# Order of the first loads, attention stages and last weight units in a hybrid decoder layer

## The chip, the cores and the metric

The kernel runs on one core of a Trainium2 chip. A core has a matrix engine (TensorE, PE in the profile, with its weight loads as PEld), three engines for elementwise work (VectorE or DVE, ScalarE or ACT, GpSimd or POOL), and SyncE (SP), which here issues nearly all transfers from HBM. Each engine works through its own list of instructions in order; between engines semaphores carry the dependences. The metric is the time of the kernel on the device in microseconds, lower is better.

## The reference

One decoder layer on x of 256 positions by 2048 channels, all in float32. Cut to what matters:

```python
h = rmsnorm(x, pre_mix_g)
q_a, k_a, v_a, q_b, k_b, v_b, f_b = jnp.split(h @ w_in, cuts, axis=-1)
o_a = swa_sink_attention(q_a, k_a, v_a, sinks)       # 16 heads, 2 kv heads, window 128, ALiBi
o_b = forgetting_attention(q_b, k_b, v_b, log_sigmoid(f_b + b_forget))   # 16 heads
mix = concat([rmsnorm(o_a, grp_swa_g), rmsnorm(o_b, grp_fox_g)]) @ w_out
x = x + rmsnorm(mix, post_mix_g)
h = rmsnorm(x, pre_ffn_g)
u = causal_dwconv(h @ w_up, conv_w, conv_b)          # width 3, 11264 channels
gate, val = jnp.split(u, 2, axis=-1)
x = x + rmsnorm((gelu(gate) * val) @ w_down, post_ffn_g)
```

## The kernel before, in words

**Precision.** Every matmul is done in three passes on numbers that are split in two: a rounded high part (`whi`, written by ACT) and the remainder (`wlo`, written by DVE as raw minus high). Activations are split the same way (`hT`, `G`, `oT`: columns 0 to 255 high, 256 to 511 low). The products are high by high, high by low and low by high.

**Weights.** A weight unit is 512 KB: `w_load` (line 64) starts its transfer on SyncE into one of four `raw` buffers, `w_split` (line 83) makes `whi` and `wlo` from it, five buffers each. `w_high` (line 69) does the same with the low part put off, for the places where the order is written by hand. `proj_T` (line 170) runs a projection of 256 output columns over four units; each unit is 8 matmuls of 512 columns and 8 of 256, and calls `tick` twice. `mm3` (line 197) is the three passes of the other kind of product, for one 128-row tile `t` of the positions.

**Order.** PE's instructions run in the order in which the program issues them. The other engines are put in order by a scheduler, except where an instruction is pinned (`keep_in_program_order`) or where a stretch is set to manual for ACT, DVE and POOL (line 653 to the end of `first_gate`). `later(n, f)` puts a piece of work n ticks on; it is how attention is laid among the projections.

**Start.** SyncE loads a small gain tile, then x in four chunks of 512 channels (the first in two halves), each followed by a unit of the key/value columns of group A. `x_chunk` transposes a chunk on PE and splits it into `hT`; `proj_T` with `first` then runs the key/value projection `bkv`. The squares of x for the norm are made by ACT in between. The first query projection (`g = 0`) follows as an ordinary `proj_T`. `rows_pre` turns the norm's factors into a row, by a matmul of ones with a diagonal (`row_of`, one diagonal buffer); `kv_a` makes the keys and values; both come 4 ticks after the key/value projection.

**Attention.** `attend` (line 335) handles a pair of heads in three stages, `scores` (with the softmax on DVE and ACT), `transposes` of the softmax, with the split into `ph` and `pl`, and `pv`, the product with the values. `stages` (line 457) gives their ticks, n, n + 5 and n + 7. Eight pairs of group A come first, eight of group B later, 8 ticks apart.

**Hand-over.** The output projection's second half keeps the units of its last two column chunks (`kept[2]`, in the common weight buffers, and `kept[3]`, in four buffers of their own), so that position tile 0 can be finished (`mix_rstd`, `residual`, `turn`: transposes to `hT`) while tile 1 is still being multiplied. `out_cols` runs a kept chunk for one tile; `gate_unit` fetches the four units of the MLP's first gate projection; `first_gate` runs it, `one(t, u)` for tile t and unit u. `ffn_tables` makes the norm's row for the MLP.

**End.** The down projection runs over four column chunks of 11 units in each half. In the last chunk of the second half the last 3 units multiply tile 0 first and tile 1 after it. `down` adds to `y_sb`, sums the squares and multiplies by the gain; at the end each tile gets its factor, is added to `x_sb` and is stored, all from SyncE.

## Time and profile before

| what | us |
|---|---|
| median of 3 runs (1118.9 to 1120.0) | 1119.46 |
| the profiled execution | 1118.4 |
| its span, first to last instruction | 1116.7 |
| PE busy | 1088.4 |
| DVE busy | 750.7 |
| ACT busy | 630.6 |
| POOL busy | 189.0 |

The span is what the trace covers; the execution's own time has another 1.7 us around it. Busy time is a union over an engine's instructions; matmuls overlap their neighbours, so PE counts as busy also where a short gap stands between two starts. In rows of the timeline the columns are start, length, engine, line, operation, output <- inputs, and in brackets the idle time of the engine before it and what ended it. In the list of waits they are total, number and longest.

### The profile page before, as it was taken

What the parts mean: (1) busy time and instruction counts of PE and PEld (TensorE: products, weight loads), DVE (VectorE), ACT (ScalarE), POOL (GpSimd) and SP (SyncE); (2) the same over time, 40 slices, a digit from 0 to 9 for tenths busy, and PEclk for the clock granted to TensorE, in tenths of its full rate; (3) what the DMA queues carried; (4) which work ended last, traced back from release to release, by engine and by line L of the source; (5) the groups of instructions that cost most, each with busy time, mean ns of one, the idle gap of its engine ahead of it and who ended that gap; (6) DMA issues with size and microseconds to landing.
All of it is one profiled execution on the core that took longest, in us unless ns stands there. A gap on an engine that the chain in (4) does not pass through costs nothing.

```text
span 1116.7 us, 15954 instructions
## 1 busy us (share of the span) xinstructions
PE 1088.4 (97%) x5846; PEld 932.0 (83%) x5846; DVE 750.7 (67%) x1141; ACT 630.6 (56%) x1077; POOL 189.0 (17%) x271
## 2 busy tenths in 40 slices
PE   8999999999999999999999999999999999999995
PEld 6779988888888888888888888888888888888884
DVE  5868787888566876767676544456777677755553
ACT  6656676667555765656565444455656565644440
POOL 4333215442013111010101000001111111101111
PEclk9999999999999999999999999999999999999998
DMA  7734466554763556565656665656565655666552
GB/s 235 223 99 129 141 197 186 168 165 152 254 208 122 175 188 196 183 195 181 196 182 194 186 189 187 189 186 191 186 192 187 191 186 190 187 228 188 189 168 76
DMA packets 164842, 202.87 MB, mean 182 GB/s; under 512 B 6780, under 2 KB 130716, under 8 KB 164252
## 3 DMA queue, kind: packets, MB, share of 16 engines
q1 hardware_dynamic: 164368, 201.67, 57.5%
q8 instruction: 46, 0.75, 0.3%
q14 instruction: 32, 0.26, 0.1%
q10 hardware_dynamic: 396, 0.18, 0.1%
HBM read 199.58 MB, written 2.11 MB: 181 GB/s over the span
## 4 chain that ended last, share of the span: by engine, by line
PE 86%; DVE 5%; ACT 4%; issue 2%; POOL 1%; DMA 1%; SPq 0%; DVEq 0%; POOLq 0%; ACTq 0%
PE bank_acc L201 31%; PE bank_acc L180 21%; PE bank_att L180 13%; PE bank_acc L185 11%; PE bank_att L185 7%; DVE wlo L89 1%; ACT whi L88 1%; PE bank_att L348 1%; PE bank_att L397 1%; DVE pl L205 1%; DMA x_in<-in_x_dram 1%; PE bank_att L399 0%; ACT hT L626 0%; DVE y_sb L855 0%; PE bank_att L350 0%
## 5 line engine op out<-in xcount | busy, mean ns | idle before, releaser
L89 DVE TENSOR_TENSOR wlo<-raw,whi 128x1024 fp32r<-128x1024 f32 (+2 forms) x360 | 452.7, 1258 | 259.4 <-ACT whi L88 258.8
L88 ACT CAST whi<-raw 128x1024 fp32r<-128x1024 f32 (+2 forms) x360 | 371.0, 1032 | 272.7 <-PE bank_acc L201 141.1
L180 PE MATMUL bank_acc<-hT,whi 128*128 128x512 f32 x1152 | 295.7, 394 | 0.0
L180 PEld LDWEIGHTS bank_acc<-hT,whi 128*128 128x128 f32 x1152 | 206.1, 189 | 35.9 <-ACT whi L88 0.4
L201 PE MATMUL bank_acc<-whi,G 128*128 128x512 f32 x704 | 221.7, 395 | 0.0
L185 PEld LDWEIGHTS bank_acc<-hT,wlo 128*128 128x128 f32 x1152 | 156.9, 191 | 10.3
L185 PE MATMUL bank_acc<-hT,wlo 128*128 128x256 f32 x1152 | 161.9, 284 | 0.0
L180 PE MATMUL bank_att<-hT,whi 128*128 128x512 f32 x640 | 161.9, 392 | 0.0
L201 PEld LDWEIGHTS bank_acc<-whi,G 128*128 128x128 f32 x704 | 132.4, 188 | 31.9
L739 POOL TENSOR_TENSOR u<-u,rowf 128x256 f32<-128x256 f32 x88 | 55.4, 651 | 550.2 <-DVE u L738 545.5
L201 PE MATMUL bank_acc<-wlo,G 128*128 128x512 f32 x352 | 139.2, 396 | 0.0
L180 PEld LDWEIGHTS bank_att<-hT,whi 128*128 128x128 f32 x640 | 115.1, 189 | 20.6
L185 PEld LDWEIGHTS bank_att<-hT,wlo 128*128 128x128 f32 x640 | 87.3, 190 | 6.2
L185 PE MATMUL bank_att<-hT,wlo 128*128 128x256 f32 x640 | 89.2, 282 | 0.0
L201 PE MATMUL bank_acc<-whi,oT 128*128 128x512 f32 (+1 forms) x272 | 83.5, 384 | 0.0
L201 PEld LDWEIGHTS bank_acc<-wlo,G 128*128 128x128 f32 x352 | 66.2, 188 | 16.0
L201 PEld LDWEIGHTS bank_acc<-whi,oT 128*128 128x128 f32 x272 | 50.2, 188 | 10.6 <-ACT whi L75 0.3
L201 PE MATMUL bank_acc<-wlo,oT 128*128 128x512 f32 (+1 forms) x136 | 52.0, 382 | 1.0 <-DVE wlo L78 1.0
L201 PE MATMUL bank_acc<-whi,hT 128*128 128x384 f32 (+1 forms) x192 | 47.6, 322 | 0.0
L737 ACT COPY cs<-bank_acc 128x256 f32<-128x256 f32 x48 | 15.9, 373 | 32.7 <-PE bank_acc L180 32.7
L201 PEld LDWEIGHTS bank_acc<-whi,hT 128*128 128x128 f32 x192 | 33.7, 188 | 0.0
L201 PEld LDWEIGHTS bank_acc<-wlo,oT 128*128 128x128 f32 x136 | 25.6, 188 | 6.3 <-DVE wlo L78 1.3
(205 smaller groups left out, 992.6 us busy)
## 6 DMA issues: line engine op xcount, KB each, us to landing
raw<-in_w_up_dram SPq DMA_DIRECT2D x176, 512.0 KB, 3.5
raw<-in_w_down_dram SPq DMA_DIRECT2D x88, 512.0 KB, 4.7
raw<-in_w_in_dram SPq DMA_DIRECT2D x52, 512.0 KB, 3.7
raw<-in_w_out_dram SPq DMA_DIRECT2D x32, 512.0 KB, 4.2
raw<-in_w_in_dram SPq DMA_DIRECT2D x16, 384.0 KB, 3.2
raw<-in_w_in_dram SPq DMA_DIRECT2D x8, 272.0 KB, 2.8
cb<-c_dram SPq DMA_DIRECT2D x8, 256.0 KB, 3.6
x_sb<-in_x_dram SPq DMA_DIRECT2D x2, 1024.0 KB
```

The lines of the kernel that those rows point to most:

```text
L88: i1 = act.copy(hi[:, :n], raw[:, :n])
L89: i2 = dve.tensor_tensor(lo[:, :n], raw[:, :n], hi[:, :n].bitcast(F32), op=ALU.subtract)
L180: pe.matmul(b, hi[:, a, m * P:(m + 1) * P], hT[:, kt, :], start=(kt == 0), stop=(kt == KT - 1))
L185: pe.matmul(b[:, 256:512], lo[:, a, m * P:(m + 1) * P], hT[:, u * 4 + a, 0:256], start=False, stop=False)
L201: pe.matmul(b, a, r[:, cols], start=(first and i == 0), stop=(last and i == 2))
L205: dve.tensor_tensor(lo, src, hi.bitcast(F32), op=ALU.subtract)
L348: pe.matmul(s1, a[:, P:256], b, start=(n == 0), stop=(n == 2))
L397: pe.matmul(ov, values(hl, 0), p[:, :, 0:256], start=(n == 0), stop=False)
L737: act.copy(c, b[:, 256:512])
L739: pool.tensor_tensor(u[:, 2:258], u[:, 2:258], rowf, op=ALU.mult)
```

## The change

Four places change, beside helpers that only carry a new argument.

1. **Start.** The gain tile is loaded by ACT's queue. The first x chunk and the first key/value unit are loaded in halves that alternate; then come the first query unit and, for each further chunk, x, its key/value unit and its query unit, in pinned order. Key/value and first query projections run side by side, unit by unit: the key/value unit, then the transposes of the next x chunk, then the query unit. The key/value accumulators use banks of the attention's tag. There are two diagonal buffers, and the diagonals are made as soon as the factors are there. `warm_up(4)` becomes `warm_up(2)`.
2. **Attention.** The stages are n, n + 6 and n + 9. Group A's first scores stand 6 ticks after the queries, not 4; group A's norm comes at tick 16, not 12.
3. **Hand-over.** The own buffers hold chunk 2 and the common ones chunk 3; tile 1 is multiplied with chunk 3 first, then with chunk 2 in two halves. The low parts of the gate units and of the transposed tile are put in another order, and `one(0, 2)` stands ahead of tile 1's transposes.
4. **End.** In the last chunk six units (`HOLD`) feed tile 0 alone at first; two of them are split into buffers of their own. Tile 1's last chunk is accumulated in two halves of 256 columns in two banks, and the order from there on is written out. The sum of squares without the last part is made ahead; tile 1's stores alternate between SyncE's and ACT's queue, the last piece in 256 columns.

The core of the diff:

```diff
-        for cs in ((slice(0, 256), slice(256, 512)) if c == 0 else
-                   (slice(c * 512, (c + 1) * 512),)):
-            sp.dma_start(x_in[:, :, cs], xv[:, :, cs])
-        first.append(w_load(w_rows(w_in, c * 4, 4, 1024, 256), 4, 256))
+    for i in range(2):
+        cs = slice(i * 256, (i + 1) * 256)
+        tc.keep_in_program_order(sp.dma_start(x_in[:, :, cs], xv[:, :, cs]))
+        tc.keep_in_program_order(
+            sp.dma_start(head[:, i * 512:(i + 1) * 512].rearrange("p (a c) -> p a c", a=2),
+                         w_rows(w_in, i * 2, 2, 1024, 256)))
+    first[0].append((head, 4, 256))
+    first[1].append(w_load(w_rows(w_in, 0, 4, 0, 256), 4, 256, True))
+
+    def first_load(c):
+        cs = slice(c * 512, (c + 1) * 512)
+        tc.keep_in_program_order(sp.dma_start(x_in[:, :, cs], xv[:, :, cs]))
+        for i, c0 in enumerate((1024, 0)):
+            first[i].append(w_load(w_rows(w_in, c * 4, 4, c0, 256), 4, 256, True))
...
+        x_part(0, (0,))
+        warm_up(2)
+        bkv = [bank("att"), bank("att")]
+        bq0 = [bank(), bank()]
+        for u in range(4):
+            parts = w_split(first[0][u], True, None if u else lambda: x_part(0, (1,)))
+            if u < 2:
+                first_load(u + 2)
+            unit_T(parts, u, bkv, False, u == 0)
+            if u:
+                x_square((2, 3, 2)[u - 1])
+            parts = w_split(first[1][u], True)
+            if u == 0:
+                x_square(1)
+            if u < 3:
+                x_part(u + 1, (0, 1))
+            else:
+                for t in range(2):
...
+                    rpre.append(rstd_of(st, D, f"rpre{t}"))
+                    dpre.append(diag_of(rpre[t]))
+                later(2, rows_pre)
+            unit_T(parts, u, bq0)
...
         def stages(n):
-            return n, n + 5, n + 7
+            return n, n + 6, n + 9
...
-        later(4, kv_a)
+        kv_a()
...
-                swa_pair(2 * g + m, q_pair(b2[m]), stages(4 + 8 * (2 * g + m) - 8 * g))
+                swa_pair(2 * g + m, q_pair(b2[m]), stages(6 + 8 * (2 * g + m) - 8 * g))
...
-        later(12, lambda: group_rstd(0, rstd_a))
+        later(16, lambda: group_rstd(0, rstd_a))
...
-                (hi, lo), low = w_high(raw, hp if n == 3 else None)
+                (hi, lo), low = w_high(raw, (hp, 4) if n == 2 else None)
...
-        b12 = out_cols(2, 1, whole)
-        pairs = [turn(0, 0), turn(0, 1)]
-        for high, _ in pairs:
+        b13 = out_cols(3, 1, whole)
+        turns = [turn(0, 0), turn(0, 1)]
+        for high, _ in turns:
             high()
-        evac_b(1, 2, b12)
+        evac_b(1, 3, b13)
         lows[0]()
-        for _, low in pairs:
+        for _, low in turns:
             low()
-        evac_b(1, 3, out_cols(3, 1, slice(0, 256)), 0)
-        for high, low in (turn(0, 2), turn(0, 3)):
+        evac_b(1, 2, out_cols(2, 1, slice(0, 256)), 0)
+        lows[1]()
+        turns = [turn(0, 2), turn(0, 3)]
+        for high, _ in turns:
             high()
-            low()
-        evac_b(1, 3, out_cols(3, 1, slice(256, 512)), 1)
+        turns[0][1]()
+        evac_b(1, 2, out_cols(2, 1, slice(256, 512)), 1)
+        turns[1][1]()
         mix_rstd(1)
-        lows[1]()
         for n in range(4):
             residual(1, n)
-        lows[2]()
...
-                rffn.append(rstd_of(st2, D, f"rffn{t}"))
+                dffn.append(diag_of(rstd_of(st2, D, f"rffn{t}")))
...
+            one(0, 2)
+            for high, low in [turn(1, u) for u in range(4)]:
                 high()
                 low()
-            one(0, 2)
             one(0, 3)
+            lows[2]()
...
+        for u in range(FHALF // 2):
+            hi, lo = w_unit(w_rows(w_down, FHALF + u * 2, 2, 1536, 512), 2, 512,
+                            keep=(fp, HOLD - 4) if LAST <= u < FHALF // 2 - 4 else None)
+            for a in range(2):
+                k = u * 2 + a
+                args = (k, hi[:, a, :], lo[:, a, :])
+                held.append(args)
+                mm3(b0, G[k], 0, *args[1:], slice(0, 512), k == 0, k == FHALF - 1)
+                for h in range(2 if u < LAST else 0):
+                    mm3(b1[h][:, halves[h]], G[k], 1, *args[1:], halves[h], k == 0, False)
...
+        v = before_last(0, 3)
+        down(0, 3, b0)
+        r = rstd_y(0, 3, v)
+        for n in range(4):
+            finish(0, slice(n * 512, (n + 1) * 512), r, sp)
+        last = fp.tile([P, 256], F32, tag="last", name="last")
+        for h in range(2):
+            if h:
+                v = before_last(1, 4)
+            for k, hi, lo in held[LAST * 2:]:
+                mm3(b1[h][:, halves[h]], G[k], 1, hi, lo, halves[h], False, k == FHALF - 1)
+            down(1, 3, b1[h], h, last if h else None)
+        r = rstd_y(1, 4, v)
+        for i, n in enumerate((512, 512, 512, 256, 256)):
+            c = (0, 512, 1024, 1536, 1792)[i]
+            finish(1, slice(c, c + n), r, (sp, act)[i % 2], last if i == 4 else None)
```

Three places show what the numbers and helpers do to the engines' orders. On PE at the start of the program, of the kernel before, from the second x chunk on (`bank_acc<-hT,whi` is a high pass of the key/value projection):

```order
L225 MATMUL bank_att<-ident,x_in 128x128 x8
L180 MATMUL bank_acc<-hT,whi 128x512 x6
L185 MATMUL bank_acc<-hT,wlo 128x256 x8
L180 MATMUL bank_acc<-hT,whi 128x512 x2
```

The same engine in the changed kernel, from the second half of x chunk 0 on (`bank_att<-hT` is the key/value projection here, `bank_acc<-hT` the queries'):

```order
L260 MATMUL bank_att<-ident,x_in 128x128 x4
L203 MATMUL bank_att<-hT,whi 128x512 x4
L208 MATMUL bank_att<-hT,wlo 128x256 x4
L203 MATMUL bank_att<-hT,whi 128x512 x2
L208 MATMUL bank_att<-hT,wlo 128x256 x4
L203 MATMUL bank_att<-hT,whi 128x512 x2
L260 MATMUL bank_att<-ident,x_in 128x128 x8
L203 MATMUL bank_acc<-hT,whi 128x512 x6
L208 MATMUL bank_acc<-hT,wlo 128x256 x8
```

Before, the first unit of keys and values stood behind the transposes of chunk 1; now it stands ahead of them, in two halves, and a query unit follows them.

On DVE behind the first pair's transposes, of the kernel before (`pl` is the low part of the transposed softmax, `oT` the evacuated value product, `t1s`, `nm` the next pair's scores and row maxima):

```order
L205 TENSOR_TENSOR pl<-bank_att,ph 128x384 x2
L89 TENSOR_TENSOR wlo<-raw,whi 128x1024
L408 SCALAR_TENSOR_TENSOR oT_116<-bank_att,gcol,oT_116 64x256 x2
L353 TENSOR_TENSOR t1s<-bank_att,t1s 128x512
L354 TENSOR_TENSOR t0s<-bank_att,t0s 128x256
L357 TENSOR_REDUCE nm<-t1s 128x2
L358 TENSOR_REDUCE nm<-t0s 128x2
```

And in the changed kernel:

```order
L240 TENSOR_TENSOR pl<-bank_att,ph 128x384 x2
L399 TENSOR_TENSOR t1s<-bank_att,t1s 128x512
L400 TENSOR_TENSOR t0s<-bank_att,t0s 128x256
L403 TENSOR_REDUCE nm<-t1s 128x2
L404 TENSOR_REDUCE nm<-t0s 128x2
L100 TENSOR_TENSOR wlo<-raw,whi 128x1024
L410 TENSOR_TENSOR nm<-nm,nsnk 128x4
L411 TENSOR_TENSOR es<-nm,snk 128x4
L454 SCALAR_TENSOR_TENSOR oT_115<-bank_att,gcol,oT_115 64x256
```

The evacuation of a pair's value product has moved from ahead of the next pair's scores into that pair's softmax.

On DVE at the hand-over, of the kernel before, from the first half of tile 1's last chunk on (`hT` rows are the low parts of a transposed tile, `x_sb` the residual, the `wlo` rows the gate's low splits):

```order
L595 SCALAR_TENSOR_TENSOR mix_sb<-bank_acc,rg_3370,mix_sb 128x256
L631 SCALAR_TENSOR_TENSOR hT_3639<-bank_att,gcol,hT_3639 128x128 x8
L595 SCALAR_TENSOR_TENSOR mix_sb<-bank_acc,rg_3370,mix_sb 128x256
L609 TENSOR_REDUCE st_m<-msq_3478 128x1
L140 TENSOR_SCALAR rv<-st_m 128x1
L78 TENSOR_TENSOR wlo<-raw,whi 128x1024
L614 SCALAR_TENSOR_TENSOR x_sb<-mix_sb,rmix_3920,x_sb 128x512 x4
```

And in the changed kernel:

```order
L645 SCALAR_TENSOR_TENSOR mix_sb<-bank_acc,rg_3389,mix_sb 128x256
L87 TENSOR_TENSOR wlo<-raw,whi 128x1024
L681 SCALAR_TENSOR_TENSOR hT_3640<-bank_att,gcol,hT_3640 128x128 x4
L645 SCALAR_TENSOR_TENSOR mix_sb<-bank_acc,rg_3389,mix_sb 128x256
L681 SCALAR_TENSOR_TENSOR hT_3640<-bank_att,gcol,hT_3640 128x128 x4
L659 TENSOR_REDUCE st_m<-msq_3479 128x1
L163 TENSOR_SCALAR rv<-st_m 128x1
L664 SCALAR_TENSOR_TENSOR x_sb<-mix_sb,rmix_3922,x_sb 128x512 x4
```

The low split has moved ahead of the last quarter's evacuation, four of the eight low parts behind it, and nothing stands between the factor's sum and the residual.

More of the change, by code (lines that the diff above doesn't have):

```diff
@@ L26 @@
 FHALF = 22
+HOLD = 6
 @with_exitstack
@@ L71, in w_high @@
+    def w_high(unit, keep=None):
         raw, a, c = unit
         n = a * c
-        hi = (pool_ or wp).tile([P, UNIT], F32R, tag="whi", bufs=4 if pool_ else 5, name="whi")
-        lo = (pool_ or wp).tile([P, UNIT], F32R, tag="wlo", bufs=4 if pool_ else 5, name="wlo")
-        act.copy(hi[:, :n], raw[:, :n])
+        hi, lo = w_parts(n, keep)
+        act.copy(hi, raw[:, :n])
         def low():
-            dve.tensor_tensor(lo[:, :n], raw[:, :n], hi[:, :n].bitcast(F32), op=ALU.subtract)
-        return (hi[:, :n].rearrange("p (a c) -> p a c", a=a),
-                lo[:, :n].rearrange("p (a c) -> p a c", a=a)), low
@@ L83, in w_split @@
-    def w_split(unit, pin=False):
+            dve.tensor_tensor(lo, raw[:, :n], hi.bitcast(F32), op=ALU.subtract)
+        return [x.rearrange("p (a c) -> p a c", a=a) for x in (hi, lo)], low
+    def w_split(unit, pin=False, between=None, keep=None):
         raw, a, c = unit
         n = a * c
-        hi = wp.tile([P, UNIT], F32R, tag="whi", bufs=5, name="whi")
-        lo = wp.tile([P, UNIT], F32R, tag="wlo", bufs=5, name="wlo")
-        i1 = act.copy(hi[:, :n], raw[:, :n])
-        i2 = dve.tensor_tensor(lo[:, :n], raw[:, :n], hi[:, :n].bitcast(F32), op=ALU.subtract)
-        if pin:
-            tc.keep_in_program_order(i1)
-            tc.keep_in_program_order(i2)
-        return (hi[:, :n].rearrange("p (a c) -> p a c", a=a),
-                lo[:, :n].rearrange("p (a c) -> p a c", a=a))
@@ L166, in row_of, with unit_T, high, low @@
         return bk[:, 0:256]
-    def proj_T(w, c0, banks, loaded=None, before=None, pin=False):
+    def unit_T(parts, u, banks, ticks=True, halves=False):
+        hi, lo = parts
+        def high(a):
+            kt = u * 4 + a
+            for m, b in enumerate(banks):
+                pe.matmul(b, hi[:, a, m * P:(m + 1) * P], hT[:, kt, :], start=(kt == 0),
+                          stop=(kt == KT - 1))
+        def low(a):
+            for m, b in enumerate(banks):
+                pe.matmul(b[:, 256:512], lo[:, a, m * P:(m + 1) * P],
+                          hT[:, u * 4 + a, 0:256], start=False, stop=False)
+        high(0)
+        high(1)
+        if halves:
+            low(0)
+            low(1)
+        high(2)
+        if ticks:
+            tick()
+        for a in range(2 if halves else 0, 4):
+            low(a)
+        high(3)
+        if ticks:
+            tick()
@@ L171, in proj_T @@
+    def proj_T(w, c0, banks, before=None, pin=False):
         for u in range(4):
-            unit = loaded[u] if loaded else w_load(w_rows(w, u * 4, 4, c0, 256), 4, 256)
-            hi, lo = w_split(unit, pin and u > 0 or loaded)
+            parts = w_split(w_load(w_rows(w, u * 4, 4, c0, 256), 4, 256), pin and u > 0)
             if before:
                 before(u)
-            def high(a):
-                kt = u * 4 + a
-                for m, b in enumerate(banks):
-                    pe.matmul(b, hi[:, a, m * P:(m + 1) * P], hT[:, kt, :], start=(kt == 0),
-                              stop=(kt == KT - 1))
@@ L789, in first_gate @@
             return banks
-        ysq = [small.tile([P, 4], F32, tag=f"ysq{t}", bufs=1, name=f"ysq{t}") for t in range(2)]
+        ysq = [small.tile([P, 5], F32, tag=f"ysq{t}", bufs=1, name=f"ysq{t}") for t in range(2)]
         gbf = None
```

161 lines of the change are left out of this document (85 added, 76 removed).

## The prediction

> **What bounds the kernel now.** I read the page first, then busy time by stage, then the waits of PE, then the timeline at each place where PE stands still.
>
> ```profile
> span 1116.7 us, 15954 instructions
> PE 1088.4 (97%) x5846; PEld 932.0 (83%) x5846; DVE 750.7 (67%) x1141; ACT 630.6 (56%) x1077; POOL 189.0 (17%) x271
> ```
>
> ```profile
> 0.00:39.40 39.40, 33.77 (x180) 26.46 (x181) 24.80 (x41) 26.36 (x52) 19.09 (x40) 0.96 0.76 236
> 39.40:158.00 118.60, 112.34 (x676) 102.10 (x675) 93.27 (x196) 77.02 (x185) 33.84 (x39) 1.00 0.49 147
> 158.00:290.00 132.00, 131.48 (x730) 111.45 (x730) 106.00 (x186) 88.17 (x195) 49.61 (x74) 1.00 0.54 168
> 290.00:386.00 96.00, 92.07 (x506) 78.15 (x505) 62.69 (x101) 55.54 (x109) 19.81 (x22) 1.00 0.61 199
> 386.00:1104.80 718.80, 718.75 (x3762) 613.84 (x3760) 458.43 (x611) 382.76 (x536) 64.89 (x94) 1.00 0.59 185
> 1104.80:1116.70 11.90, 0.00 (x0) 0.00 (x0) 5.54 (x10) 0.72 (x2) 1.77 (x2) 0.59 0.49 176
> ```
>
> TensorE is busy for 97% of the span. Columns are the stretch, its length, then PE, PEld, DVE, ACT, POOL busy, clock, DMA share and GB/s. From 386 to 1104.8 us PE is busy for 718.75 of 718.80 us, and the change leaves those matmuls alone, except in the last weight column. All that can be won lies in the other five rows: the start, the two attention rows, the hand-over to the MLP, and 11.9 us after the last matmul. The waits of PE name the places (total, times, longest):
>
> ```profile
> PE bank_att L386 <- DVE t0s L376: 3.7, 3, 1.9
> PE bank_att L225 <- DMA x_in<-in_x_dram: 3.1, 1, 3.1
> PE bank_att L165 <- DVE diag L164: 2.5, 2, 1.3
> PE bank_att L397 <- DVE pl L205: 2.4, 3, 1.1
> PE bank_att L621 <- DVE x_sb L614: 1.7, 1, 1.7
> ```
>
> **The start: 5.2 us.** One weight unit of a transposed projection (8 wide and 8 narrow matmuls) takes 1.84 + 0.95 = 2.79 us:
>
> ```profile
> 161.50 1.84 PE bank_acc L180 x8
> 163.34 0.95 PE bank_acc L185 x8
> ```
>
> ```profile
> 9.96 1.09 PE L225 MATMUL bank_att<-ident,x_in 128*128 128x128 f32 x8 [3.11 <-DMA x_in<-in_x_dram]
> ...
> 38.95 2.00 PE L180 MATMUL bank_acc<-hT,whi 128*128 128x512 f32 x8
> ```
>
> ```profile
> 10.00:20.00 10.00, 10.00 (x57) 8.93 (x58) 6.38 (x11) 6.08 (x14) 4.93 (x7) 0.83 0.93 294
> GB/s 0 5 124 336 148 284 320 367 371 388 349 367 384 363 314 176 346 187 321 137 0 123 362 55 3 220 323 216 315 302 179 44 314 244 264 255 253 264 147 329
> ```
>
> Keys/values and the first queries are 8 units. Before, the second one ends with the first two matmuls of the row at 38.95, so at 39.4 us; some 1.0 us of that is small work that stays (gain rows, diagonals, value transposes): 38.4. Of the changed kernel, x and both projections are 6.3 MB. The second line gives GB/s for each us. x chunk 1 ended the first 1.57 MB of the list before and was landed by 9.96 us; now 2.1 MB end with it: 0.52 MB more at 350 to 370 GB/s is 1.4 us later, less about 0.45 us because the tiny gain load (a SyncE issue of that length) leaves the queue: 10.9 us. Unit 0 of keys/values runs before that, in two halves, on data landed by about 8 us. Behind chunk 1, PE has three transposed chunks (0.87 us each: 8 at 0.109, by the row at 9.96, whose last one runs on for 0.27) and seven units: 2.6 + 19.5 + 0.2 for joints = 22.3, done at 33.2. That is 38.4 - 33.2 = **5.2 us**. No unit waits on its own chunk: between a chunk's transposes and the unit that uses it stands the query unit of the chunk before, 2.79 us. ACT then has per chunk 1.57 (hT) + 2.1 (casts) + 0.87 a square, 5.4 to 6.3 us beside PE's 6.46; that cover is thin, and where it fails some tenths appear. SyncE gets a new wait: the load of keys/values unit 2 needs the first raw buffer, and behind it stand query unit 2, x chunk 3 and all later weights; that buffer is free near 10 us, chunk 3 then lands near 16, and PE wants it near 23. Bounds: chunk 1 landed at 9.5 (same place as before, less the gain load) gives 6.6; landed at 12.2 (0.52 MB at the row's mean of 234) gives 3.9; half clock once more costs 1.7 (below).
>
> Row 10 to 20 us has clock 0.83: after the idle 3.1 us TensorE ran half as fast for some 3.4 us, 1.7 us lost. My chain has no PE gap over 1.2 us before 11 us, so I charge none. The Trainium skill, "TensorE: Matmul & The Clock Gate", Part 1, says that the clock is halved after an idle window of about 3.4 us of a free-running counter, and its Part 4 that transposes do not count as activity in the same way. By that second rule the stretch from 4 to 8 us, which is warm-up, transposes and a small start on unit 0, could count as idle and the sum would lose 1.7 us again; before, a similar stretch kept full clock.
>
> **Attention: 7.7 us.** The sixteen pairs each put scores, transposes of the softmax and the product with the values on PE at ticks of about 1.4 us (half a unit).
>
> ```profile
> 45.00 0.40 PE L348 MATMUL bank_att<-keys,qh 128*128 128x512 f32 x1
> ...
> 53.65 0.47 DVE L376 TENSOR_SCALAR t0s<-t0s,rs 128x128 f32<-128x128 f32 x2
> ...
> 203.32 0.63 PE L397 MATMUL bank_att<-ph,vpb 128*128 128x512 f32 x2
> 204.05 0.50 PE L397 MATMUL bank_att<-pl,vpb 128*128 128x512 f32 x1
> ```
>
> Waits for the softmax (3.7) and for pl (2.4) are 6.1 us of idle PE; each of the six hides 0.16 more, as a matmul of 0.39 us is followed at a pitch of 0.23: 1.0. Five forget-gate pairs lose 204.05 - 203.32 - 0.47 = 0.26 each without showing idle: 1.3; two small ones at 85 and 100 us about 0.5. Together 8.9. The normalised softmax came 54.1 - 45.0 = 9.1 us after the scores, with 8.0 us of PE work ahead. Now 6 ticks stand there, 8.4 + 1.05 for the scores = 9.45, and from the second pair on also the previous pair's value product, 1.05: 10.5. So the softmax waits should go, even if that product's evacuation (two DVE instructions of some 0.45, four on ACT) now falls into the next softmax: 9.1 + 0.9 = 10.0. The third tick behind the transposes adds 1.4 us, and the next scores another 1.05, where the largest wait for pl was 1.1. What stays: pair 0, with no product ahead and the queries' evacuation 2 ticks behind its scores, 0.5; pair 6, whose ticks are 1.0 us, 0.3; and the first scores, which now stand 9.2 us behind the diagonals and must have keys that come by way of GpSimd, a copy through the queue and ACT, 0.4 (an estimate). 8.9 - 1.2 = **7.7**. Bounds: 8.9, and 3 if DVE, busy 93.3 of 118.6 us there, gives half of it back.
>
> **Hand-over to the MLP: 4.0 us.**
>
> ```profile
> 360.66 1.60 DVE L78 TENSOR_TENSOR wlo<-raw,whi 128x1024 fp32r<-128x1024 f32 x1
> ...
> 361.14 1.53 POOL L142 TENSOR_TENSOR rmix<-rv,mhalf 128x1 f32<-128x1 f32 x1
> ...
> 363.51 2.64 PE L621 MATMUL bank_att<-ident,x_sb 128*128 128x128 f32 x16 [1.70 <-DVE x_sb L614]
> ...
> 381.57 0.49 PE L165 MATMUL bank_att<-diag,ones 128*128 128x128 f32 x2 [1.21 <-DVE diag L164]
> ```
>
> The transposes of tile 1 wait 1.7 us for the residual and then trickle at its pace, 2.64 us for 1.74 (16 at 0.109). Ahead of that, DVE was behind with the last quarter's evacuation: eight low parts of about 0.27 us stood before it; now four do, some 1.0 us. The 1.60 us low split leaves the place between the sum and the residual, and while it ran the power on GpSimd took 1.53 us; I take back 0.9 of that (an estimate, from the 0.55 of the same line where DVE was idle). So the residual starts 1.9 us earlier, and PE has eight more matmuls, one(0,2), 0.96 us, ahead of the transposes, which then run at once: 2.5 us won. Both diagonals are now made before PE asks for them (second near 376.9, asked for near 377.5): 1.5 us. The 1.0 us wait on the kept low split at 342 us stays, as the square ahead of that cast stays. Bounds: 1.5 (one of the two) to 4.5.
>
> **The end: 3.0 us.**
>
> ```profile
> 1103.95 2.74 DVE L855 SCALAR_TENSOR_TENSOR y_sb<-y_sb,ry,x_sb 128x512 f32<-128x512 f32 x4 [1.53 <-POOL ry L142]
> ...
> 1106.61 0.68 DVE L828 TENSOR_TENSOR y_sb<-bank_acc,y_sb 128x512 f32<-128x512 f32 x1
> ...
> 1109.99 2.74 DVE L855 SCALAR_TENSOR_TENSOR y_sb<-y_sb,ry,x_sb 128x512 f32<-128x512 f32 x4 [1.50 <-POOL ry L142]
> ```
>
> ```profile
> 352.59 0.28 PE L201 MATMUL bank_acc<-wlo,oT 128*128 128x256 f32 x1
> 352.71 0.40 PE L201 MATMUL bank_acc<-whi,oT 128*128 128x256 f32 x2
> ```
>
> Tile 1's first sum is ready at 1109.99 + 0.69 = 1110.68, 5.9 us after PE, 1.8 of them because DVE still finishes tile 0 (the addition starts only at 1106.61); the output then takes 6.01 us. Now tile 0 has 72 narrow matmuls of cover, 8.6 us, for its 6.1 us chain. After the last matmul: addition of 256 columns 0.47, square and read-out 0.5, one small sum 0.16, power 0.55, first residual 0.69, hand-overs 0.2: 2.5. Since 1 MB still has to leave, I keep the 6.0: 8.5 instead of 11.9, 3.4 won. 66 wide matmuls become 132 narrow ones; a narrow one starts 0.12 us after the one before it, a wide one 0.233 (8 in 1.84 and a hand-over), so 132 x 0.12 - 66 x 0.233 = 0.4 lost. **3.0**, bounds 2 to 3.6. Weights for the six units that feed tile 0 alone (1.4 us each, 512 KB) are loaded ahead; nine units of buffers hide that, and I charge nothing (bound 1).
>
> **Sum.** 5.2 + 7.7 + 4.0 + 3.0 = 19.9. The profiled execution took 1118.4 us (span 1116.7 and 1.7 around it): 1098.5. The median of the runs shown, 1119.46, is 1.1 higher: 1099.6, say **1099.5**.
>
> **Rivals.** (1) Waits come back as DVE and ACT run nearer to full in the first 160 us: the start wins 3.5 and attention 3.5, 1105.4. For: DVE is busy 79% there; against: it idles in every stretch. (2) The clock halves again at the start, because too little of a 3.4 us stretch before 11 us is matmul: 1.7, 1101.2; the row of 10 to 20 us shows that it can, and a denser start speaks against it. (3) Slower than before: each next pair's softmax is pushed behind the previous pair's evacuation. It decides from 10.5 us between scores and softmax; at 12.2 for all sixteen, 1.7 x 16 = 27 us lost against 12.2 won elsewhere, 1134. Against: 9.1 was the most seen, forget pairs had slack. (4) Little happens, as each wait is handed on to a later one: 1118; against: 386 to 1104.8 shows PE waits for nothing there.
>
> **Chances.** Forecast 0.62 (1095.5 to 1102), clock 0.13, rival 1 0.18, no change 0.03, slower 0.04. All low bounds together would be 1112, all high ones 1096. Range 1095 to 1107, 0.85 of it. A measurement tells about 0.2% (2.2 us) from no change: faster 0.93, same 0.03, slower 0.04.
>
> **What would show it.** Right: first queries done near 33 us, clock 1.00 from 10 to 20; no PE wait for softmax or pl over 0.5 us; no wait of the transposes for x_sb or of the row for its diagonal; 8.5 us behind the last matmul. Wrong: PE waiting for casts or the chunk transposes before 33 us, or new waits of transposes near 10.5 us behind the scores.

## The result, and the profile after

| | before | after |
|---|---|---|
| median of the runs, us | 1119.61 (4 runs, 1118.9 to 1120.0) | 1103.12 (4 runs, 1100.63 to 1104.05) |
| ratio of the medians | | 0.985, 95% interval 0.9831 to 0.9869 |
| profiled execution (span), us | 1118.4 (1116.7) | 1102.26 (1100.5) |

The kernel became 1.5% faster. The forecast was 1099.5 in a range of 1095 to 1107; the measured median lies in the range, but 3.6 us above the forecast, outside the 1095.5 to 1102 that had most of the chance, and 2.3 us below the 1105.4 of rival 1. The forecast sum was 19.9 us; the spans differ by 16.2. Where the 3.7 us are missing is the question of the rest.

The head of the page of the changed kernel, then its busy time by stage; columns are the stretch, its length, PE, PEld, DVE, ACT and POOL busy, clock, DMA share and GB/s:

```profile
span 1100.5 us, 16111 instructions
PE 1083.3 (98%) x5910; PEld 935.0 (85%) x5910; DVE 751.6 (68%) x1146; ACT 630.8 (57%) x1080; POOL 196.0 (18%) x272
```

```profile
0.00:33.30 33.30, 31.69 (x172) 25.14 (x173) 19.50 (x36) 24.47 (x49) 16.64 (x38) 1.00 0.76 243
33.30:142.00 108.70, 104.87 (x640) 97.11 (x639) 91.03 (x182) 72.18 (x173) 36.78 (x40) 1.00 0.52 157
142.00:274.00 132.00, 130.32 (x738) 111.98 (x737) 109.09 (x199) 90.05 (x205) 54.71 (x74) 1.00 0.55 172
274.00:370.00 96.00, 94.97 (x523) 81.34 (x522) 62.34 (x101) 58.32 (x113) 17.29 (x21) 1.00 0.58 194
370.00:1091.20 721.20, 721.20 (x3843) 619.38 (x3843) 466.06 (x625) 385.26 (x541) 69.11 (x97) 1.00 0.58 188
1091.20:1100.50 9.30, 0.28 (x3) 0.08 (x1) 3.54 (x7) 0.51 (x2) 1.45 (x3) 0.76 0.33 114
```

The reader looks at length minus PE busy. The start now idles 1.6 us (5.6 before), the hand-over 1.0 (3.9), the middle nothing, the end 9.0 (11.9). The two attention rows still idle 3.8 and 1.7 us; before it was 6.3 and 0.5. The stretches don't hold quite the same work, so the rows only point to the place.

For equal work I use single instructions that exist in both kernels: the end of the first queries, the matmul behind the one wait that stayed (kept low split of the output projection), and the last matmul. Timeline of PE, before:

```profile
342.31 0.50 PE L201 MATMUL bank_acc<-wlo,oT 128*128 128x512 f32 x1 [1.01 <-DVE wlo L78]
...
1104.36 0.40 PE L201 MATMUL bank_acc<-whi,G 128*128 128x512 f32 x1
```

And after:

```profile
33.26 0.60 PE L191 MATMUL bank_att<-diag,ones 128*128 128x128 f32 x4
...
333.26 0.50 PE L236 MATMUL bank_acc<-wlo,oT 128*128 128x512 f32 x1 [1.03 <-DVE wlo L87]
...
1091.21 0.28 PE L236 MATMUL bank_acc<-whi,G 128*128 128x256 f32 x1
```

The kept split's wait ends 9.05 us earlier, the last matmul starts 13.15 us earlier, the span ends 16.2 us earlier. The first queries end at 33.26 (38.4 before, without the small work that stays). So:

| part | forecast, us | measured, us |
|---|---|---|
| start: 38.4 - 33.26 | 5.2 | 5.1 |
| attention: 9.05 - 5.1 | 7.7 | 3.9 |
| hand-over and narrow matmuls: 13.15 - 9.05 | 4.0 - 0.4 | 4.1 |
| end: 16.2 - 13.15 | 3.4 | 3.05 |

Three parts came as forecast and one came half. PE's waits of the changed kernel say why (total us, times, longest):

```profile
PE bank_att L432 <- DVE t0s L422: 3.8, 2, 2.4
...
PE bank_att L590 <- POOL sqs L460: 1.1, 1, 1.1
PE bank_acc L236 <- DVE wlo L87: 1.0, 1, 1.0
PE bank_att L394 <- ACT keys L239: 0.6, 1, 0.6
PE bank_att L203 <- DVE hT L178: 0.2, 1, 0.2
PE bank_att L208 <- DVE wlo L100: 0.2, 1, 0.2
```

All waits for pl are gone, and those for x_sb, the diagonals and chunk 1. But two transposes wait for their softmax, 1.4 us at pair 0 and 2.4 at pair 6, where I had left 0.5 and 0.3. Two waits are new: the group norm's matmul for the square sum on GpSimd (1.1) and the first forget-gate scores for their keys (0.6). Together that is 5.5 us.

**The 1.4 us: pair 0.** Timeline of DVE of the changed kernel; pair 0's scores run on PE from 42.69 to 43.91:

```profile
42.43 0.87 DVE L240 TENSOR_TENSOR keys<-scr,keys 64x256 fp32r<-64x256 f32 x2
...
45.21 1.22 DVE L100 TENSOR_TENSOR wlo<-raw,whi 128x1024 fp32r<-128x1024 f32 x1
46.35 0.68 DVE L399 TENSOR_TENSOR t1s<-bank_att,t1s 128x512 f32<-128x512 f32 x1
```

DVE takes the scores up 2.4 us after they are done (0.3 in the kernel before): splits of the keys and the values, a copy of gains and two low splits stand ahead of them. From the start of the scores to the end of the softmax it is 11.1 us instead of 9.1.

**The 2.4 us: pair 6.** Its scores start at 124.60; the transposes come at 135.28, 10.7 us later, while the narrow matmuls ahead of them are done at 132.9. Timeline of ACT of the changed kernel there:

```profile
123.54 0.87 ACT L239 CAST ph<-bank_att 128x384 fp32r<-128x384 f32 x2
127.81 1.05 ACT L99 CAST whi<-raw 128x1024 fp32r<-128x1024 f32 x1 [3.40 <-DMA raw<-in_w_in_dram]
130.36 1.05 ACT L99 CAST whi<-raw 128x1024 fp32r<-128x1024 f32 x1 [1.51 <-DMA raw<-in_w_in_dram]
131.32 0.46 ACT L452 ACTIVATE oT<-bank_att,gcol 64x256 fp32r<-64x256 f32 x1
131.68 0.50 ACT L415 ACTIVATE t1s<-t1s,nm 128x256 f32<-128x256 f32 x1
```

ACT stands still for 4.9 us, on two casts whose weights are still being loaded. Pair 6's exponentials (L415) are queued behind them. On DVE the last step that they need (L410, at 130.03) stands in turn behind the low split of the first of these casts.

**The 1.1 and 0.6 us: group norm and keys.** Timeline of POOL of the changed kernel:

```profile
159.66 0.48 POOL L492 TENSOR_SCALAR t1f<-cb,cq 128x256 f32<-128x256 f32 x1 [4.09 <-DMA cb<-c_dram]
...
164.48 0.73 POOL L460 TENSOR_TENSOR sqs<-sqs,sqo 128x256 f32<-128x256 f32 x1
...
167.05 2.06 POOL L165 TENSOR_TENSOR rg<-rv,mhalf 128x1 f32<-128x1 f32 x2
169.09 1.42 POOL L365 TENSOR_TENSOR scr<-scr 128x256 f32<-128x256 f32 x2
```

POOL first waits for the cumulative sums, which go through memory (cb from c_dram), makes the mask tables of the first two forget-gate pairs from 159.66 on, fits pair 7's square sum between them, then does the norm's two powers, and only then scales the keys (L365). PE waits at two points of this row.

### The profile page after: what moved, and what is told of

The parts are those of the page before. It is cut to its first block, busy times and chain, and to the rows that moved or that the text cites. A ratio compares the mean times of both kernels' runs of the same rounds, so it can differ in the third digit from the quotient of the medians.

```text
span 1100.5 us, 16111 instructions
## 1 busy us (share of the span) xinstructions
PE 1083.3 (98%) x5910; PEld 935.0 (85%) x5910; DVE 751.6 (68%) x1146; ACT 630.8 (57%) x1080; POOL 196.0 (18%) x272
## 4 chain that ended last, share of the span: by engine, by line
PE 92%; DVE 2%; ACT 1%; POOL 1%; DMA 1%; issue 1%; DVEq 0%; POOLq 0%; ACTq 0%
PE bank_acc L236 33%; PE bank_acc L203 21%; PE bank_att L203 14%; PE bank_acc L208 11%; PE bank_att L208 7%; PE bank_att L394 1%; PE bank_att L443 1%; DVE wlo L100 1%; PE bank_acc L823 1%; DMA raw<-in_w_in_dram 1%; PE bank_acc L819 0%; PE bank_att L396 0%; PE bank_att L445 0%; POOL scr L365 0%; DMA cb<-c_dram 0%
## 5 line engine op out<-in xcount | busy, mean ns | idle before, releaser
L100 DVE TENSOR_TENSOR wlo<-raw,whi 128x1024 fp32r<-128x1024 f32 (+3 forms) x361 | 454.4, 1262 | 250.2 <-ACT whi L99 249.9
L99 ACT CAST whi<-raw 128x1024 fp32r<-128x1024 f32 (+3 forms) x361 | 370.7, 1030 | 273.4 <-PE bank_acc L236 133.2
L203 PE MATMUL bank_acc<-hT,whi 128*128 128x512 f32 x1120 | 286.5, 393 | 0.0
L203 PEld LDWEIGHTS bank_acc<-hT,whi 128*128 128x128 f32 x1120 | 200.0, 189 | 34.5
L236 PE MATMUL bank_acc<-whi,G 128*128 128x512 f32 (+1 forms) x748 | 223.0, 382 | 0.0
L203 PE MATMUL bank_att<-hT,whi 128*128 128x512 f32 x672 | 170.8, 392 | 0.2 <-DVE hT L178 0.2
L208 PEld LDWEIGHTS bank_acc<-hT,wlo 128*128 128x128 f32 x1120 | 151.4, 190 | 9.5
L236 PE MATMUL bank_acc<-wlo,G 128*128 128x512 f32 (+1 forms) x374 | 142.7, 382 | 0.0
L203 PEld LDWEIGHTS bank_att<-hT,whi 128*128 128x128 f32 x672 | 120.7, 189 | 21.8 <-ACT whi L99 0.4
L236 PEld LDWEIGHTS bank_acc<-whi,oT 128*128 128x128 f32 x272 | 50.2, 188 | 10.5 <-ACT whi L84 0.2
L882 POOL TENSOR_TENSOR y_sb<-y_sb,gbc_ffn 128x512 f32<-128x512 f32 (+1 forms) x8 | 12.6, 1589 | 107.8 <-ACT junk L881 107.8
```

The source lines that it names most:

```text
L99: i1 = act.copy(hi[:, cs], raw[:, cs])
L100: i2 = dve.tensor_tensor(lo[:, cs], raw[:, cs], hi[:, cs].bitcast(F32), op=ALU.subtract)
L203: pe.matmul(b, hi[:, a, m * P:(m + 1) * P], hT[:, kt, :], start=(kt == 0), stop=(kt == KT - 1))
L208: pe.matmul(b[:, 256:512], lo[:, a, m * P:(m + 1) * P], hT[:, u * 4 + a, 0:256], start=False, stop=False)
L236: pe.matmul(b, a, r[:, cols], start=(first and i == 0), stop=(last and i == 2))
L882: pool.tensor_tensor(ys if into is None else into, ys, gbf[:, n * 512:(n + 1) * 512][:, cs], op=ALU.mult)
```

## The experiments

All changes are made to the changed kernel. Each was timed in four or five runs beside the kernel before, whose median was 1118.2 to 1118.5 in these sessions; so the ratio with its interval stands beside each time. The changed kernel's are 1103.12 and 0.985 (0.9831 to 0.9869). The last column is read from the one profiled execution of each: the time from the end of the first queries to the end of the wait at the kept low split, which holds both groups of attention. It is 303.9 us before (counted from 38.4) and 300.0 in the changed kernel.

| run | median, us | ratio to before (95%) | attention, us |
|---|---|---|---|
| 1 attention stages back | 1110.19 | 0.9929 (0.9914 to 0.9944) | 307.7 |
| 2 norm at 20 ticks | 1102.07 | 0.9860 (0.9840 to 0.9880) | 299.3 |
| 3 pairs 0 and 6 two ticks later | 1101.16 | 0.9846 (0.9831 to 0.9861) | 298.1 |
| 4 one more raw buffer | 1101.98 | 0.9855 (0.9841 to 0.9869) | 299.5 |
| 5 shift taken back | 1099.73 | 0.9836 (0.9822 to 0.9849) | 297.6 |
| 6 shift and stages back | 1109.18 | 0.9919 (0.9905 to 0.9932) | 306.2 |
| 7 as 5, pair 0 later | 1099.98 | 0.9837 (0.9824 to 0.9851) | 297.8 |
| 8 three units kept at the end | 1106.47 | 0.9896 (0.9882 to 0.9909) | 301.4 |
| 9 pair 6's wait filled | 1105.25 | 0.9882 (0.9869 to 0.9896) | 303.0 |
| 10 as 5, norm at 24 | 1098.68 | 0.9825 (0.9811 to 0.9838) | 297.1 |
| 11 as 5, pairs 0 and 7 later, keys first | 1097.14 | 0.9809 (0.9796 to 0.9822) | 295.0 |
| 12 as 5, old hand-over | 1103.12 | 0.9863 (0.9849 to 0.9876) | 297.7 |

The intervals of runs 2, 3 and 4 overlap the changed kernel's for the most part, and by the ratio 2 and 4 are no faster than it. What these three show is where PE waits in the profile, not a gain that is clear of noise; the same holds for 6 against 1 and for 7 and 10 against 5. The expectations count a wait some 0.16 us longer than the waits view does (1.6 for 1.43 at pair 0), because matmuls usually overlap by that much.

### 1. The attention part alone undone

```diff
-            return n, n + 6, n + 9
+            return n, n + 5, n + 7
...
-        later(16, lambda: group_rstd(0, rstd_a))
+        later(12, lambda: group_rstd(0, rstd_a))
```

> The later stages put back to 5 and 7 ticks behind the scores and the first group norm to 12 ticks, all else as in the changed kernel (1103.1 us). Theory A (the attention part of the change was worth 3.9 us here, because four waits of 1.6, 2.6, 1.25 and 0.75 us took the place of those removed): about 1107.0, and PE's waits for the normalised softmax and for pl are back at pairs 0 to 2, together some 6 us with those of pair 6. Theory B (the attention part was worth the predicted 7.7 us and the shortfall lies in another part): about 1110.8.

Measured 1110.19, 7.1 us above the changed kernel, close to theory B. The waits view of PE of this run:

```profile
PE bank_att L432 <- DVE t0s L422: 8.4, 5, 2.7
```

The kernel before waited 3.7 us in three places here; with the new start and the old stages it is 8.4 in five. Both theories were too simple. Here the later stages are worth about what I forecast for them (7.1 by the medians, 8.0 by the spans), but they take away other losses than the ones that I had summed up. The attention nevertheless came out only 3.9 better than before, because the rest of the change made it 3.8 us worse first (307.7 against 303.9): the losses that I had counted on the kernel before were not those that the new start left.

Busy time of this run around the longest of these waits shows a second cost:

```profile
51.00:53.70 2.70, 0.19 (x1) 0.00 (x0) 2.47 (x7) 2.54 (x9) 1.52 (x1) 1.00 0.83 223
53.70:57.10 3.40, 3.17 (x15) 3.20 (x16) 2.77 (x6) 1.16 (x3) 1.86 (x3) 0.51 0.38 105
57.10:60.50 3.40, 3.40 (x20) 2.95 (x19) 1.23 (x1) 1.41 (x2) 1.09 (x2) 0.99 0.26 94
```

Behind a wait of 2.7 us, at pair 0, the clock is 0.51 for 3.4 us: another 1.7 us lost, which is a part of the 3.8. Experiment 9 returns to this.

### 2 to 4. The four waits, one by one

Only the norm's tick, 16 to 20:

> Only the first group norm is moved, from 16 to 20 ticks. Theory A (PE waits 1.25 us at 164 us because the square sum of pair 7 stands on GpSimd behind the tables of the first forget-gate pair, and the keys of that pair come 0.75 us late because DVE and GpSimd stand behind this norm): both waits go, 1101.1. Rival (DVE and GpSimd are just too full there): the 1.25 us go, but the wait of the first forget-gate scores grows by as much, 1103.1; halfway, with the keys' wait staying at 0.75, 1101.9.

Measured 1102.07; one of the four runs took 1106.0. The norm's wait went; the keys' wait grew from 0.6 to 1.5 us. The rival came closer: POOL's row stays as late as before, only PE meets it at another point.

Pairs 0 and 6 with their transposes and product two ticks later:

```diff
-            return n, n + 6, n + 9
+            return n, n + 6 + more, n + 9 + more
...
-                swa_pair(2 * g + m, q_pair(b2[m]), stages(6 + 8 * (2 * g + m) - 8 * g))
+                swa_pair(2 * g + m, q_pair(b2[m]), stages(6 + 8 * (2 * g + m) - 8 * g, {0: 2, 6: 2}.get(2 * g + m, 0)))
```

> Only pairs 0 and 6 get their transposes and value product two ticks later (8 and 11). Theory A (these two softmaxes are late for reasons of their own place, 1.6 and 2.6 us of PE waits; all others have 2 to 4 us to spare): both waits go and none comes in their place, 4.1 us less: 1099.0. Rival (DVE and ACT run too full before 160 us, so that what PE does not wait for here it waits for at the next pair): new waits of the same size at pairs 1, 2 and 7, within 1 us of 1103.1.

Measured 1101.16: 2.0 of 4.1 us by the medians, 1.9 by the last column. Both softmax waits went, 3.8 us, and the 0.6 at the forget-gate keys. In their place came 0.8 us for pl of pair 6, 1.0 for pair 7's softmax, and the norm's wait grew from 1.1 to 1.7. Half of what is won comes back within 30 us.

One more raw buffer for every second unit of the last value columns:

```diff
+                if cols == 272 and u % 2:
+                    raw = ap.tile([P, 544], F32, tag="rawv", bufs=1, name="raw")
+                    sp.dma_start(raw.rearrange("p (a c) -> p a c", a=2),
+                                 w_rows(w_in, u * 2, 2, c0, cols))
+                    hi, lo = w_split((raw, 2, cols))
...
```

> One more raw buffer for the last eight units of the value projection, so that the loads of the next projection are issued earlier; stages as in the changed kernel. Theory A1 (the wait of 2.6 us at pair 6 comes from ACT, which stands 3.4 and 1.5 us on two casts whose weights are still on their way, with the exponentials of pair 6 queued behind them): the idle of ACT in front of these casts shrinks below 1.5 us in all and the wait at pair 6 falls below 0.5 us, 2.1 or more less: 1100.9. Rival A2 (the softmax of pair 6 is late because there are only 7.7 us of narrow matmuls ahead of it, whatever the loads do): the wait stays at 2 us or more, 1103.

Measured 1101.98. Timeline of ACT of this run at the same place, then two lines of its PE waits:

```profile
128.48 0.65 ACT L99 CAST whi<-raw 128x544 fp32r<-128x544 f32 x1 [4.54 <-DMA raw<-in_w_in_dram]
129.03 0.20 ACT L412 ACTIVATE es<-es 128x4 f32<-128x4 f32 x1
129.14 0.50 ACT L415 ACTIVATE t1s<-t1s,nm 128x256 f32<-128x256 f32 x1
```

```profile
PE bank_att L596 <- POOL sqs L460: 3.1, 1, 3.1
PE bank_att L432 <- DVE t0s L422: 1.3, 1, 1.3
```

The wait at pair 6 is gone without a tick more ahead of it, so A2 falls: there is time enough. But not for the reason I gave. ACT still waits 4.5 us for a load; only one late cast, not two, now stands ahead of the exponentials, which start at 129.1 instead of 131.7. What decides is what the exponentials are queued behind. And the 2.4 us won turn up at the norm, whose wait grows by 2.0.

### 5 and 6. The shift of two ticks

With the new start, the first eight pairs moved two ticks against the projections. Here pair 0 stays at 6, pair 1 comes one tick and all others two ticks earlier:

```diff
-                swa_pair(2 * g + m, q_pair(b2[m]), stages(6 + 8 * (2 * g + m) - 8 * g))
+                swa_pair(2 * g + m, q_pair(b2[m]), stages((6, 5, 4)[min(2 * g + m, 2)] + 8 * (2 * g + m) - 8 * g))
```

> The first scores of the pairs again 4 ticks behind the projection before them from pair 2 on (pair 0 at 6, pair 1 at 5 + 8); transposes and value product stay 6 and 9 ticks behind. Theory C (the shift of all pairs by two ticks, which came with the new start, is what cost: it put pair 6's transposes at the last tick of the value projection and pair 7 and the group norm among the first forget-gate tables): the wait at pair 6 falls from 2.6 to about 0.5 us, the 1.25 us of the group norm go, the keys of the first forget-gate pair are then up to 2 us late because their tables come by way of a round trip through memory: 1100.5. Rival D (that round trip sets the time from 150 to 170 us by itself, whatever is won ahead of it): the keys' wait grows by all that is won, 1102.5 to 1103.

Measured 1099.73, and the four runs lie within 0.14 us. PE's waits:

```profile
PE bank_att L432 <- DVE t0s L422: 2.5, 2, 1.3
...
PE bank_att L394 <- ACT keys L239: 0.8, 1, 0.8
```

Pair 6's wait and the norm's are gone; pair 7 waits 1.2 us instead. By the spans of the profiled executions it is 2.5 us better (1098.0 against 1100.5), by the medians 3.4, by the ratios 1.6; the intervals of the two ratios overlap. By the waits, theory C came out; D did not. Pair 0, which this edit leaves at 6, still waits 1.3 us.

The same with the old stages:

> As the kernel before this in the list, but with the old stages (5 and 7 ticks, group norm at 12), so that only the shift differs from the kernel with the attention stages put back (1110.2 us). Theory C: the waits of 1.55 at pair 5 and 1.76 at pair 7 go, the rest stays: 1106.9. If the shift has no part in it: 1110.2.

Measured 1109.18, 1.0 below experiment 1 where 3.3 was expected:

```profile
PE bank_att L432 <- DVE t0s L422: 5.8, 3, 2.7
PE bank_att L443 <- DVE pl L240: 1.4, 2, 1.1
```

Pairs 5 and 7 wait no more, as expected, but two waits for pl come back, and the 2.7 us of pair 0 and 1.9 at pair 6 stay; behind the latter the clock is 0.50 for 3.4 us (137.3 to 140.7). So the shift is not the whole of the 3.8 us. By the last column it is 1.5 of them, and a halved stretch is 1.7. Pair 0, which with the same stages waited 0.8 us in the kernel before, is a part of its own; here it is partly made up for by shorter waits for pl.

### 7. Pair 0, two ticks later

> The kernel with the shift taken back from pair 2 on, and pair 0's transposes and product two ticks later. Theory A (pair 0's softmax is late by 1.6 us for DVE work of its own place and nothing follows from it): 1.5 less than without, about 1099. Rival (the 1.5 us come back at a later wait): the same as without.

Measured 1099.98: nothing won, the rival. The wait of the transposes went, but the value product, two ticks later too, waited 1.2 us for ph and pl.

### 8. The end with three units kept

`HOLD = 6` becomes 3.

> Three units kept for tile 1 at the end in place of six, all else as in the changed kernel (1103.1 us). Theory (the 72 narrow matmuls, 8.5 us, are there to cover the 6.2 us from tile 0's last matmul to its last residual; 36 of them, 4.25 us, don't): tile 1's additions stand behind tile 0's residuals on DVE, the stretch behind the last matmul grows from 9.3 to about 12 us: 1105.8. Rival (the stretch behind the last matmul is set by the stores, whose last one takes 4.2 us from its issue): below 1 us more, 1104.

Measured 1106.47. Timeline of DVE of this run, whose last matmul starts at 1092.59:

```profile
1092.17 2.74 DVE L916 SCALAR_TENSOR_TENSOR y_sb<-y_sb,ry,x_sb 128x512 f32<-128x512 f32 x4 [1.71 <-POOL ry L912]
1094.83 0.41 DVE L880 TENSOR_TENSOR y_sb<-bank_acc,y_sb 128x256 f32<-128x256 f32 x1
...
1098.03 2.47 DVE L916 SCALAR_TENSOR_TENSOR y_sb<-y_sb,ry,x_sb 128x512 f32<-128x512 f32 x4 [0.66 <-POOL ry L912]
```

Tile 1's first addition stands behind tile 0's residuals. From the start of the last matmul to the end (span 1105.1) it is 12.5 us where the changed kernel has 9.3: the theory, with 3.2 us. This profile also has a clock of 0.50 from 136.3 to 139.7 us, behind a wait of 2.3 at pair 6, which has nothing to do with the end: up to there this kernel is the changed one, and its last column is 1.4 us longer.

### 9. The wait at pair 6 filled

```diff
+                if j == 6:
+                    fill = bank("att")
+                    for _ in range(10):
+                        pe.matmul(fill, junk[:, 0:P], junk, start=True, stop=True)
```

> The changed kernel (1103.1 us, single runs from 1100.6 to 1104.05) with ten matmuls on the zeroed scratch tile, 2.3 us at full clock, put into PE's wait of 2.6 us ahead of pair 6's transposes; their result is not used. Theory (in some runs that wait lets the clock halve for 3.4 us behind it, 1.7 us lost, which is the spread of the changed kernel): no run with a halved stretch behind 130 us, all runs within 1 us, and the time at that of the better runs of the changed kernel, 1100.5 to 1101.5. Rival (the spread comes from the phase in which the clock rises in the first 8 us): spread as before, about 1102 to 1103.

Measured 1105.25; the expected time was wrong. The four runs lie within 1.1 us, so the first 8 us don't spread them by more than that, against the rival; but they all lie high. In the profile the clock holds behind pair 6. The norm's wait grows to 2.7 us, and the halving moves there:

```profile
163.00:166.00 3.00, 0.34 (x2) 0.19 (x2) 0.00 (x0) 1.54 (x3) 2.75 (x7) 0.87 0.13 42
166.00:169.40 3.40, 3.40 (x11) 2.82 (x12) 2.04 (x5) 0.00 (x0) 2.30 (x3) 0.50 0.89 237
```

It lasts longer here: the clock is 0.50 from 165.3 to 172.1 us, 6.8 us. PE is at work for 6.3 of these, so some 3 us are lost, which is about what the last column has lost against the changed kernel (303.0 against 300.0). So with pair 6's wait filled, a longer halving came at another wait; whether a halved stretch makes the spread of the changed kernel is not shown by this run.

### 10. The norm behind the keys

As 5, with the norm at 24 ticks.

> The kernel with the shift taken back from pair 2 on (1099.7 us), with the first group norm at 24 ticks in place of 16. Theory (its two powers, 2.06 us on GpSimd, stand ahead of the scaling of the first forget-gate keys, and PE waits 0.94 us for these keys): the wait goes, 1098.8. Rival (the tables of the second forget-gate pair, which stand there too, are enough to keep the keys late): no change, 1099.7.

Measured 1098.68, the expected time; but the keys' wait falls from 0.8 to 0.3 us, not to nothing, and the last column by 0.5. The other half of the 1.0 us between the two profiles lies ahead of the attention, which this edit does not touch: the first queries end at 32.74 instead of 33.26. So the time was met in part by luck.

### 11. Every remaining wait by its own cause

As 5, with:

```diff
-            return n, n + 6, n + 9
+            return n, n + 6 + more[0], n + 9 + more[1]
...
+                swa_pair(2 * g + m, q_pair(b2[m]), stages((6, 5, 4)[min(2 * g + m, 2)] + 8 * (2 * g + m) - 8 * g,
+                                                        {0: (2, 3), 7: (1, 1)}.get(2 * g + m, (0, 0))))
...
-        later(16, lambda: group_rstd(0, rstd_a))
+        later(18, lambda: group_rstd(0, rstd_a))
```

and with the scaling of the first keys and the second pair's tables kept in program order on POOL.

> The kernel with the shift taken back from pair 2 on (1099.7 us), and: pair 0's transposes and product 2 and 3 ticks later, pair 7's 1 and 1, the group norm at 18, and on GpSimd the scaling of the first forget-gate keys ahead of the tables of the second pair. Theory (each remaining wait has its own local cause): 1.5 at pair 0, 1.3 at pair 7 and 0.9 at the keys go, 1096.0. Rival (DVE and ACT are too full before 170 us, what goes here comes back there): 1099 to 1099.7.

Measured 1097.14, the best of all, its interval below the changed kernel's. PE's waits, and POOL's timeline at the keys:

```profile
...
PE bank_acc L236 <- DVE wlo L87: 1.0, 1, 1.0
PE bank_att L400 <- DVE oT L458: 0.9, 1, 0.9
PE bank_att L203 <- DVE hT L178: 0.6, 1, 0.6
```

```profile
162.20 2.41 POOL L369 TENSOR_TENSOR scr<-scr 128x256 f32<-128x256 f32 x2
166.51 1.71 POOL L165 TENSOR_TENSOR rg<-rv,mhalf 128x1 f32<-128x1 f32 x2 [1.90 <-DVE rv L163]
```

The keys are scaled at 162.2 instead of 169.1, ahead of the powers. No transposes wait for a softmax, the norm and the keys are not waited for. One wait of 0.9 us is new, of scores near 67 us for a bank that a value product still holds (its evacuation oT releases them). DVE is busy for 753.2 us (751.6 in the changed kernel), so the same load can be put in an order without these waits. By the last column the attention now wins 8.9 us over the kernel before (295.0 against 303.9), the whole of the 8.9 that the prediction had found there. This run moved four things together; it does not say what each is worth.

### 12. The hand-over alone undone

As 5, with chunk 2 first for tile 1, chunk 3 in halves, `lows[1]()` ahead of the residual and `one(0, 2)` behind the transposes, as before the change; the diagonals stay early.

> The kernel with the shift taken back from pair 2 on (1099.7 us), with the old order of the hand-over: chunk 2 first for tile 1, chunk 3 in halves, the low split ahead of the residual, and the third gate unit behind the transposes; the diagonals stay early. Theory (my term of 2.5 us for this part): the transposes wait 1.7 us for the residual and trickle behind it, 1102.2. Rival (the wait at the hand-over went with the diagonals and other small work): less than 1 us, 1100.5.

Measured 1103.12, 3.4 us above 5:

```profile
PE bank_att L671 <- DVE x_sb L664: 1.7, 1, 1.7
```

```profile
352.00:355.40 3.40, 3.39 (x19) 2.67 (x20) 3.40 (x7) 2.81 (x12) 0.00 (x0) 0.74 0.53 165
```

The 1.7 us wait for the residual is back as it was before the change. Behind it the clock falls, to 0.50 from about 353.6 to 357.0 us in this profile. From the kept split to the last matmul this run takes 761.9 us and experiment 5 takes 758.0: of the 3.9 us some 1.7 are the halved stretch, which leaves 2.2 for the order itself, near the 2.5 of the forecast. The 1.5 us forecast for the early diagonals have no run of their own; PE's wait of 1.2 us for the second diagonal is gone.

## Why the prediction was right, and where it was not

- **Start: right in its time, but by another path.** Forecast done at 33.2 us, measured 33.26. The prediction let the landing of x chunk 1, at 10.9 us, set the start of its transposes. They start at 11.04 and wait for no load; what is ahead of them is the first key/value unit, in which PE waits 0.2 us each for hT and for a low part. In experiment 11 the same transposes run from 10.40 and wait for no load either, so that chunk had landed by then, and that the two times agree so closely is luck. The work behind them came as forecast. The stretch to 33.3 us shows clock 1.00. Rival 2 (the clock halves again at the start) did not occur in this profile.
- **Attention: the step that failed** is "What stays: pair 0 ... 0.5; pair 6, whose ticks are 1.0 us, 0.3; and the first scores ... 0.4". Measured as idle time of PE: 1.4 at pair 0, 2.4 at pair 6 and nothing at the first scores, which are group A's; but also 1.1 for the norm and 0.6 for the first forget-gate keys, neither of which I had listed. That is 5.5 us instead of 1.2, and the term came out 3.9 instead of 7.7. The forecast of 10.0 us from scores to softmax was too long for thirteen pairs, which took 6.8 to 8.0, and too short for pairs 0, 6 and 7, which took 10.7 to 11.4. What I had not priced is that the first scores at 6 ticks instead of 4 move every pair of the group against the projections, and that with the new start DVE comes late to pair 0's scores: the losses were taken from the kernel before and assumed to stay where they were.
- **Luck in the size of the stages.** That experiment 1 gives the stages about the forecast 7.7 us (7.1 by the medians) is in part luck, since 1.7 of it is a halved stretch of that profile. Of the 3.8 us by which its attention is slower than in the kernel before, 1.7 are this stretch and 1.5 go with the shift (experiment 6). How the remainder adds up from pair 0's longer wait and the shorter ones for pl stays open.
- **Rival 1** had the right size for attention (3.5 against 3.9) and the wrong mechanism. It blamed DVE and ACT running full. Experiment 4 removes the wait at pair 6, and experiment 11 all four, with the same load, by what stands ahead of what. Only at pair 0 does its reason fit the rows: DVE has no gap over 0.2 us from 39.9 to 52 us. Its half on the start did not occur.
- **Rival 3** (slower) named the right point, 10.5 us between scores and softmax, but three pairs reached it, not sixteen, and of these pair 7 had 12.3 us ahead of its transposes and did not wait.
- **Hand-over: right.** No wait for x_sb or a diagonal is left, the 1.0 us at the kept split stayed as said, and experiment 12 brings the 1.7 us back.
- **End: right to 0.5 us.** 9.0 us behind the last matmul instead of the forecast 8.5. Timeline of DVE and ACT's queue of the changed kernel:

```profile
1093.42 2.47 DVE L916 SCALAR_TENSOR_TENSOR y_sb<-y_sb,ry,x_sb 128x512 f32<-128x512 f32 x4 [0.66 <-POOL ry L912]
1094.87 1.43 ACTq L918 DMA_DIRECT2D out_dram<-y_sb  x2
1095.82 0.48 DVE L916 SCALAR_TENSOR_TENSOR y_sb<-last,ry,x_sb 128x256 f32<-128x256 f32 x1
```

The four residuals start 1.9 us behind the last matmul's end, so the first is done after 2.6 (forecast 2.5); from there to the end it is 6.4 us instead of 6.0. Experiment 8 shows that tile 0's cover is what this part won.

## What to carry to other kernels

Losses read from the old profile belong to the old order: when an early part is moved, read off anew which work each later wait will meet, above all at the joints between projections. On an in-order engine ask first what stands ahead of the late instruction; a cast that waits for a load, or two powers on one element each, delays whatever is queued behind it, however idle the engine is. And take waits away together: one at a time, in the profiles of experiments 2, 3, 4 and 7, half or more of what was won came back at the next point of the same chain.
